# A decoder trunk on one core: 32 of the 44 chunks of the last product as seven-product pairs

## The chip, the core and the metric

The kernel runs on one core of a Trainium2 chip. Its engines are TensorE (PE, matmuls; PEld its weight loads), VectorE (DVE), ScalarE (ACT), GpSimd (POOL) and SyncE (SP); SP and POOL issue the transfers between HBM and on-chip memory, each into a queue of its own. The metric is device time in microseconds. Before: a median of 2108.53 us in three runs (2105.98 to 2113.35).

## The reference

One layer of a decoder trunk on 512 tokens of width 2048, in float32, and a last RMSNorm. The part that matters is the second half of the layer:

```python
def conv_glu_ffn(h, w_gate, w_up, conv_w, conv_b, w_down):
    g = causal_dwconv(h @ w_gate, conv_w, conv_b)
    return (jax.nn.silu(g) * (h @ w_up)) @ w_down
...
x = x + gt2 * conv_glu_ffn(h, ...)
return rmsnorm(x, final_g)
```

`D_FF` is 5632, which is 44 chunks of 128. Every value is split for TensorE into a high and a low part (float32r), and a product is three matmuls: high x high, high x low, low x high. Ahead of this half stand a conditioning vector (`w_ada`, 96 rows of 128 x 2048, each reduced on VectorE), a first RMSNorm, the mixer (pooling, attention, a recurrent branch) and its output projection `w_o`.

## The kernel before, in words

Activations lie feature-major: a tile is 128 features x 512 tokens. Stages follow one another: start, mixer, output projection, four gate/up chunks plainly (`PLAIN`), 40 gate/up pairs, the last product (`w_dn`), the last norm.

**Gate and up as pairs.** A `Pair` takes gate and up chunk i as the two row blocks of a 2 x 2 scheme: features 0 to 1023 and 1024 to 2047 are the two inner blocks, tokens 0 to 255 (`LO`) and 256 to 511 (`HI`) the two column blocks. It needs seven products of half size in place of eight: weights a11, s2, s1, s3, a12, a22, s4 (s1 to s4 are sums made on VectorE) times the forms b11, t2, t1, t3, b21, t4, b22 of the activations, which are made once and stay on chip. `pair_steps` writes the order of a pair by hand: seven windows, one product each; in a window ScalarE casts a later operand to its high part (`high`), VectorE makes the low part (`low`), and banks are copied and added (`kept`, `result`, `c21`, `c11`, `c12`). High and low parts go through a ring of four buffers each, so a cast waits for the product four earlier. The bank A is added to by four products of a pair; each addition waits for ScalarE's copy of what stood there.

**The last product.** The gated tile of each chunk is stored in HBM (`a_d`, POOL). The 44 chunks are cut in groups of 9, 13, 9 and 13 (`FFG`). For a group, each of the 16 output tiles j is one slot: SP loads its weights (`raw_d`), ScalarE and VectorE split them (`wh_d`, `wl_d`), TensorE makes 3 matmuls of 512 columns per chunk, and VectorE adds the bank times a gate into the residual x1b (`down_done`). The next group's gated tiles are loaded and split beside it. The last group runs twice, in token halves of 256 columns, so that the norm of the first half stands beside the second. `drive` loads two slots ahead. The first slot's weights are loaded as `fd_raw`.

The order within an engine is fixed when the program is built; a tile's buffer is given again when the last reader of the old content is done, and the waits follow from that.

## Time and profile before

| | |
|---|---|
| median of 3 runs | 2108.53 us |
| the profiled execution | 2111.79 us, span 2110.0 us |
| TensorE busy | 2044.6 us, 97% |
| VectorE busy | 1481.6 us, 70% |
| ScalarE busy | 879.0 us, 42% |
| granted TensorE clock, mean | 0.992 |
| moved by DMA | 358.80 MB, 170 GB/s in the mean |

Busy time is the union of an engine's instructions; a matmul's row is longer than its distance to the next one, since they are pipelined. The granted clock is given as a share of full speed. The pairs end at about 1599.5 us, and the last product runs from there to 2095.6.

### The profile page before, as it was taken

The numbers are of one execution on the slowest core, as the hardware profiler recorded it, in microseconds if no ns is written. First come the engines' busy times: TensorE is split into PE (matmuls) and PEld (weight loads), VectorE is DVE, ScalarE is ACT, GpSimd is POOL, SyncE is SP. The second block draws the span as 40 slices with busy tenths as digits, with TensorE's granted clock in tenths as the row PEclk, the third lists the DMA queues.
The fourth block names the chain that finished last, engine by engine and source line by source line (L and its number), as shares of the span: only waits on it lengthen the run. The fifth ranks groups of instructions, "written<-read, shape, count | busy, mean of one in ns | idle before, by whom it ended". The sixth has DMA issues, their size and how long they took to land.

```text
span 2110.0 us, 32077 instructions
## 1 busy us (share of the span) xinstructions
PE 2044.6 (97%) x13172; PEld 1858.4 (88%) x13172; DVE 1481.6 (70%) x1850; ACT 879.0 (42%) x1252; POOL 77.5 (4%) x135
## 2 busy tenths in 40 slices
PE   6899999999999999999999999999998999999997
PEld 3678788989877788999999999999997888888997
DVE  7987876777676757887877877878875443344675
ACT  4247432335222634544444544444544231222453
POOL 0001100002000010000000000000000000000000
PEclk9999999999999999999999999999999999999999
DMA  9963466666877235333333334334326543333564
GB/s 360 370 230 100 154 242 229 236 227 219 312 283 281 99 105 181 125 111 125 121 115 125 116 118 128 110 117 134 103 94 236 172 157 96 101 122 120 185 205 135
DMA packets 85846, 358.80 MB, mean 170 GB/s; under 512 B 9793, under 2 KB 16065, under 8 KB 68161
## 3 DMA queue, kind: packets, MB, share of 16 engines
q1 hardware_dynamic: 77442, 336.82, 47.1%
q0 software_dynamic: 8256, 19.93, 2.6%
q8 instruction: 103, 1.69, 0.3%
q14 instruction: 45, 0.37, 0.1%
HBM read 334.69 MB, written 22.02 MB: 169 GB/s over the span
## 4 chain that ended last, share of the span: by engine, by line
PE 70%; DMA 3%; DVE 1%; issue 1%; ACT 0%; DVEq 0%; SPq 0%; ACTq 0%
PE z_d L113 8%; PE z_d L114 8%; PE z_d L115 8%; PE A L938 7%; PE A L939 7%; PE A L937 7%; PE C L937 4%; PE C L938 4%; PE C L939 4%; DMA raw_ada<-in_w_ada 2%; PE B L939 2%; PE B L938 2%; PE B L937 2%; PE z_o L114 2%; PE z_o L115 2%; PE z_o L113 1%
## 5 line engine op out<-in xcount | busy, mean ns | idle before, releaser
L113 PE MATMUL z_d<-a,wh_d 128*128 128x512 f32 (+1 forms) x903 | 308.2, 341 | 0.1
L114 PE MATMUL z_d<-a,wh_d 128*128 128x512 f32 (+1 forms) x903 | 307.8, 341 | 0.0
L115 PE MATMUL z_d<-a,wl_d 128*128 128x512 f32 (+1 forms) x903 | 307.6, 341 | 0.0
L103 ACT CAST wh_d<-raw_d 128x896 fp32r<-128x896 f32 (+3 forms) x158 | 127.1, 805 | 294.1 <-PE z_d L114 293.4
L104 DVE TENSOR_TENSOR wl_d<-raw_d,wh_d 128x896 fp32r<-128x896 f32 (+3 forms) x158 | 145.2, 919 | 148.3 <-ACT wh_d L103 147.1
L126 DVE SCALAR_TENSOR_TENSOR raw_ada<-raw_ada,crep 128x2048 f32<-128x2048 f32 x64 | 147.1, 2299 | 64.8 <-DMA raw_ada<-in_w_ada 64.7
L113 PEld LDWEIGHTS z_d<-a,wh_d 128*128 128x128 f32 x903 | 171.5, 190 | 19.9 <-ACT wh_d L103 0.8
L114 PEld LDWEIGHTS z_d<-a,wh_d 128*128 128x128 f32 x903 | 171.5, 190 | 19.0
L115 PEld LDWEIGHTS z_d<-a,wl_d 128*128 128x128 f32 x903 | 171.3, 190 | 18.8
L1073 DVE SCALAR_TENSOR_TENSOR x1b<-z_d,mod,x1b 128x512 f32<-128x512 f32 (+1 forms) x80 | 51.5, 644 | 87.5 <-PE z_d L115 87.5
L928 DVE TENSOR_TENSOR s1l<-s,s1h 128x1024 fp32r<-128x1024 f32 x40 | 49.0, 1225 | 65.6 <-ACT s1h L923 65.6
L937 PE MATMUL C<-hh_b,s1h 128*128 128x256 f32 x320 | 90.5, 283 | 2.9 <-ACT s1h L923 2.9
L939 PE MATMUL A<-hh_b,a11l 128*128 128x256 f32 x320 | 90.3, 282 | 0.8 <-DVE a11l L928 0.8
L937 PE MATMUL A<-hh_b,a11h 128*128 128x256 f32 x320 | 90.3, 282 | 0.7 <-ACT a11h L923 0.7
L937 PE MATMUL A<-t42h,s2h 128*128 128x256 f32 x320 | 90.7, 283 | 0.0
L938 PE MATMUL A<-t42l,s2h 128*128 128x256 f32 x320 | 90.7, 283 | 0.0
L939 PE MATMUL A<-t42h,s2l 128*128 128x256 f32 x320 | 90.6, 283 | 0.0
L938 PE MATMUL C<-hl_b,s1h 128*128 128x256 f32 x320 | 90.3, 282 | 0.0
L939 PE MATMUL C<-hh_b,s1l 128*128 128x256 f32 x320 | 90.2, 282 | 0.0
L938 PE MATMUL C<-hl_b,s4h 128*128 128x256 f32 x320 | 90.2, 282 | 0.0
L937 PE MATMUL A<-t3h,s3h 128*128 128x256 f32 x320 | 90.2, 282 | 0.0
L939 PE MATMUL B<-hh_b,a12l 128*128 128x256 f32 x320 | 90.2, 282 | 0.0
(652 smaller groups left out, 6258.5 us busy)
## 6 DMA issues: line engine op xcount, KB each, us to landing
a<-in_w_gu SPq DMA_DIRECT2D x160, 512.0 KB, 3.8
raw_ada<-in_w_ada SPq DMA_DIRECT2D x64, 1024.0 KB, 4.9
raw_d<-in_w_dn SPq DMA_DIRECT2D x48, 832.0 KB, 4.4
ada<-in_w_ada SPq DMA_DIRECT2D x32, 1024.0 KB, 7.0
raw_d<-in_w_dn SPq DMA_DIRECT2D x31, 576.0 KB, 3.8
raw_o<-in_w_o SPq DMA_DIRECT2D x16, 1024.0 KB, 5.0
ar<-a_d SPq DMA_DIRECT2D x44, 256.0 KB, 4.7
a_d<-ac POOLq DMA_DIRECT2D x43, 256.0 KB, 3.2
```

Of the source, the lines that this page charges most:

```text
L103: A.copy(h, raw[:, a:b])
L104: V.tensor_tensor(l, raw[:, a:b], h.bitcast(F32), ALU.subtract)
L113: T.matmul(acc, wh, xh, start=start, stop=False)
L114: T.matmul(acc, wh, xl, start=False, stop=False)
L115: T.matmul(acc, wl, xh, start=False, stop=stop)
L126: V.scalar_tensor_tensor(raw, raw, 1.0, crep, op0=ALU.mult, op1=ALU.mult, accum_out=modr[:, n:n + 1])
L928: V.tensor_tensor(l, getattr(self, n), self.w[n][0].bitcast(F32), ALU.subtract)
L937: T.matmul(o, wh[:, w], xh, start=first, stop=False, skip_group_check=True)
L938: T.matmul(o, wh[:, w], xl, start=False, stop=False, skip_group_check=True)
L939: T.matmul(o, wl[:, w], xh, start=False, stop=last, skip_group_check=True)
L1073: V.scalar_tensor_tensor(x1[j][:, c], acc[:, c], mod[:, 80 + j:81 + j], x1[j][:, c], op0=ALU.mult, op1=ALU.add)
```

## The change

Chunks 4 to 35 (32 of 44) of the last product are made by the seven-product scheme too; the other twelve (`REST`: 0 to 3 and 36 to 43) stay plain and run in token halves at the end.

*Forms.* While gate and up run, two gated tiles e and e + 1 are the two inner blocks of a column of seven forms (`Forms`): ScalarE and VectorE make them three steps after chunk e, and POOL stores their high and low parts in HBM (`f_d`), 128 x (4 chunk pairs) x 2 x 256 per form and group. The gated tiles of these chunks are no longer stored.

*Pairs of the last product.* There are four groups of four chunk pairs. In a group, output tiles 2f and 2f + 1 are the two row blocks of a `Down` pair, f from 0 to 7: seven products, each 4 chunks x 3 matmuls of 256 columns. Its weights are blocks of 128 x 512: SP loads a11, a12, a22 and the first term of s1 and s3, and the second term of s1 and s3 is added by a transfer of POOL (`accum_op=ALU.add`), two pairs ahead. The residual tiles are loaded in group 0. The forms of a group are loaded by POOL, 1 MB each, into two sets of buffers (`tm.F`); those of the next group are asked for after the first pair of a group. `down_steps` has the order of `pair_steps`.

*The twelve plain chunks.* In group 3 their gated tiles are loaded and split, two per pair, into the buffers of the forms that are done with (`rest`).

*Smaller things.* Several buffers become single (`t`, `u3`, `u`, `g`), the pool of results `st.m` outlives the gate/up stage, the norm's tiles are cut to its width, the square root's table is no longer loaded ahead of the last norm, the conditioning rows are dealt out differently over the slots (three more in the value products, one fewer in zy3, four fewer in the output projection), and one pooling product moves a slot ahead.

```diff
-FFG = (9, 13, 9, 13)
+DG, DN = 4, 4
+DFIRST, DEND = PLAIN, PLAIN + 2 * DG * DN
+REST = tuple(range(DFIRST)) + tuple(range(DEND, NFF))
+FORMS = ("b11", "t3", "t2", "b21", "t1", "t4", "b22")
...
+    f_d = {(g, n): dr.tile([P, DN, 2, HS], F32R, name=f"f_d_{n}_{g}") for g in range(DG) for n in FORMS}
...
-                              ada=min(kq, 1)))
+                              ada=1))
...
-                     ada=1 if j == 0 else 0 if j >= KC - 2 else 2, post=[lambda acc, j=j: o_done(j, acc)])
+                     ada=1 if j == 1 else 2 if 1 < j < KC - 3 else 0, post=[lambda acc, j=j: o_done(j, acc)])
...
+    class Forms:
+        def __init__(self, e):
+            m = (e - DFIRST) // 2
+            self.i, self.g, self.c, self.t = e, m // DN, m % DN, {}
+            def at(step, window, f, *a):
+                extra.setdefault((e + step, window), []).append(later(f, *a))
+            at(1, 5, self.high, "w", 0, LO)
+            at(2, 0, self.low, "w", ("b11",))
+            at(2, 5, self.high, "x", 1, ALL)
+            at(3, 0, self.low, "x", ("b21", "b22"))
+            at(3, 0, self.sums)
+            at(3, 1, self.high, "y", 0, ALL)
+            at(3, 2, self.low, "y", ("t1", "t3"))
+            at(3, 3, self.high, "z", 1, ALL)
+            at(3, 5, self.low, "z", ("t4", "t2"))
+        def high(self, key, u, c):
+            v = made[self.i + u][:, c]
+            t = tm.fs.tile([P, 2, c.stop - c.start], F32R, tag="fw" if key == "w" else "fs", name=f"f{key}_{self.i}", bufs=1 if key == "w" else 2)
+            A.copy(t[:, 0], v)
+            self.t[key] = t, v
+        def low(self, key, names):
+            t, v = self.t.pop(key)
+            V.tensor_tensor(t[:, 1], v, t[:, 0].bitcast(F32), ALU.subtract)
+            for k, n in enumerate(names):
+                G.dma_start(f_d[self.g, n][:, self.c], t[:, :, k * HS:(k + 1) * HS])
+        def sums(self):
+            e, o = made[self.i], made[self.i + 1]
+            V.tensor_tensor(e[:, LO], e[:, LO], e[:, HI], ALU.subtract)
+            V.tensor_tensor(e[:, HI], o[:, HI], e[:, HI], ALU.subtract)
+            V.scalar_tensor_tensor(o[:, HI], e[:, LO], -1.0, o[:, HI], op0=ALU.mult, op1=ALU.subtract)
+            V.scalar_tensor_tensor(o[:, LO], o[:, HI], -1.0, o[:, LO], op0=ALU.mult, op1=ALU.subtract)
+    for e in range(DFIRST, DEND, 2):
+        Forms(e)
...
+    def load_forms(g, *names):
+        for n in names:
+            Ft[g, n] = tm.F.tile([P, DN, 2, HS], F32R, tag=n, name=f"F{n}_{g}")
+            G.dma_start(Ft[g, n], f_d[g, n])
+    class Down(Pair):
+        n = DN
+        def __init__(self, g, f):
+            self.grp, self.f, self.i, self.w = g, f, f"{g}_{f}", {}
+        def part(self, u, k):
+            return w_dh[2 * self.f + u][:, k, self.grp * DN * P:(self.grp + 1) * DN * P]
+        def load_part(self, n, u, k, bufs):
+            t = st.q.tile([P, DN * P], F32, tag=n, name=f"{n}_{self.i}", bufs=bufs)
+            nc.sync.dma_start(t, self.part(u, k))
+            setattr(self, n, t)
+        def load_s(self):
+            self.load_part("s1", 1, 0, 3)
+            self.load_part("s3", 0, 0, 3)
+            G.dma_start(self.s1, self.part(1, 1), accum_op=ALU.add)
+            G.dma_start(self.s3, self.part(1, 0), accum_op=ALU.add)
+        def load_a(self):
+            self.load_part("a11", 0, 0, 1)
+        def load_b(self):
+            self.load_part("a12", 0, 1, 2)
+            self.load_part("a22", 1, 1, 1)
...
+        def add(self, n, u):
+            j = 2 * self.f + u
+            m = st.neg[:, j:j + 1] if u else mod[:, 80 + j:81 + j]
+            V.scalar_tensor_tensor(x1[j], getattr(self, n), m, x1[j], op0=ALU.mult, op1=ALU.add)
+    def down_steps(p, q, q2, o):
+        q2.load_s()
+        q.load_a()
+        A_ = p.half("A")
+        p.product(A_, "a11", p.x("b11"), True)
+        p.high("s1")
+        p.low("s2")
+        o.c21()
+        o.c11()
+        o.last()
+        m1 = p.kept("m1", A_)
+        p.high("s3")
+        p.low("s1")
+        o.add("u", 1)
+        p.product(A_, "s2", p.x("t2"), False)
+        p.high("a12")
+        o.c12()
+        p.low("s3")
+        o.add("g", 0)
+        C_ = p.half("C")
+        p.product(C_, "s1", p.x("t1"), True)
+        u2 = p.kept("u2", A_)
+        p.high("a22")
+        p.low("a12")
+        p.sum4()
+        p.product(A_, "s3", p.x("t3"), False)
+        q.load_b()
+        q.high_a11()
+        p.low("a22")
+        B_ = p.half("B")
+        p.product(B_, "a12", p.x("b21"), True)
+        u3 = p.kept("u3", A_)
+        p.high("s4")
+        q.sum2()
+        q.low_a11()
+        p.product(A_, "a22", p.x("t4"), False)
+        q.high_s2()
+        p.result("u", HI, u3, C_)
+        p.low("s4")
+        p.last = lambda: p.product(C_, "s4", p.x("b22"), False)
+        p.c21 = lambda: A.copy(p.u[:, LO], A_)
+        p.c11 = lambda: p.result("g", LO, m1, B_)
+        p.c12 = lambda: p.result("g", HI, u2, C_)
+    def down_halves(before):
+        ps_ = [Down(g, f) for g in range(DG) for f in range(KC // 2)] + [ABSENT, ABSENT]
+        p = ps_[0]
+        p.load_s()
+        p.load_a()
+        load_forms(0, "b11", "t2", "t1")
+        ps_[1].load_s()
+        p.load_b()
+        load_forms(0, "t3", "b21", "t4", "b22")
+        p.high("a11")
+        p.sum2()
+        p.low("a11")
+        p.high("s2")
+        before()
+        o = ABSENT
+        for k, p in enumerate(ps_[:-2]):
+            if p.grp == 0:
+                load_x1(2 * p.f)
+                load_x1(2 * p.f + 1)
+            down_steps(p, ps_[k + 1], ps_[k + 2], o)
+            if p.f == 0 and p.grp + 1 < DG:
+                load_forms(p.grp + 1, "b11", "t2", "t1", "t3", "b21", "t4", "b22")
+            if p.grp == DG - 1:
+                rest(p.f)
+            o = p
...
+    rest_a = []
+    def rest(f):
+        if f == 0:
+            st.raw = tm.F.tile([P, 4, S], F32, tag=FORMS[-1], name="rest_raw")
+            rest_a.extend(tm.F.tile([P, 2, 2, S], F32R, tag=n, name=f"rest_{n}") for n in FORMS[:-1])
+        if f in (0, 2, 4):
+            for k in range(4):
+                nc.sync.dma_start(st.raw[:, k], a_d[REST[2 * f + k]])
+        if f < 6:
+            for k in range(2):
+                i = 2 * f + k
+                t, v = rest_a[i // 2][:, i % 2], st.raw[:, i % 4]
+                A.copy(t[:, 0], v)
+                V.tensor_tensor(t[:, 1], v, t[:, 0].bitcast(F32), ALU.subtract)
+                a_h[i], a_l[i] = t[:, 0], t[:, 1]
...
-        for g, nff in enumerate(FFG):
...
+        nr = len(REST)
...
+                s = feature_tile(w_dr[j], f"d{j}_{i}", x, range(nr), c=HALVES[i],
...
```

On POOL, at the end of gate and up, the kernel before has only the stores of the gated tiles, and nothing after them (numbers are the program's own names):

```order
L771 DMA a_d38_148<-ac38_14572 128x512 [waits DMASW6_49,DVE_49]
L771 DMA a_d39_149<-ac39_14805 128x512 [waits DMASW7_49,DVE_49]
L771 DMA a_d40_150<-ac40_15038 128x512 [waits DMASW0_49,DVE_49]
L771 DMA a_d41_151<-ac41_15271 128x512 [waits DMASW1_49,DVE_49]
L771 DMA a_d42_152<-ac42_15495 128x512 [waits DMASW2_49,DVE_49]
L771 DMA a_d43_153<-last_t_15340 128x512 [waits DMASW3_49,DVE_49]
```

In the changed kernel the forms (F, then the form, the group) and the second terms of s1 and s3 (s1, group, pair) stand there, in this order:

```order
L1136 DMA Fb11_0_15949<-f_d_b11_0_122 128x2048 [waits DMASW3_49,PE_49]
L1157 DMA s1_0_0_15941<-in_w_dh 128x512 [waits DMAHW0_49,DMASW4_49,DVE_49]
L1158 DMA s3_0_0_15943<-in_w_dh 128x512 [waits DMAHW5_49,DMAHW1_49,DMAHW6_49,DMASW5_49,Activation_49]
L1136 DMA Ft2_0_15951<-f_d_t2_0_124 128x2048 [waits DMASW6_49]
L1136 DMA Ft1_0_15953<-f_d_t1_0_126 128x2048 [waits DMASW7_49]
...
L1157 DMA s1_0_2_15991<-in_w_dh 128x512 [waits DMAHW1_49,DMASW7_49]
L1158 DMA s3_0_2_15993<-in_w_dh 128x512 [waits DMAHW2_49,DMASW0_49]
L1136 DMA Fb11_1_16117<-f_d_b11_1_129 128x2048 [waits DMASW1_49]
L1136 DMA Ft2_1_16119<-f_d_t2_1_131 128x2048 [waits DMASW2_49]
...
L1136 DMA Fb22_1_16129<-f_d_b22_1_135 128x2048 [waits DMASW7_49]
L1157 DMA s1_0_3_16135<-in_w_dh 128x512 [waits DMAHW7_49,DMASW0_49,DVE_49]
L1158 DMA s3_0_3_16137<-in_w_dh 128x512 [waits DMAHW1_49,DMASW1_49,DVE_49]
```

The first form waits for TensorE; between the parts shown stand the other forms of group 0, the sums of pair 1, one store, and four forms of group 1. The sums of pair 3 stand behind all forms of group 1.

On VectorE the kernel before has, in the second group of the last product, two low parts and one residual add per output tile:

```order
L104 TENSOR_TENSOR wl_d1_5_0_16608<-raw_d1_5_16549,wh_d1_5_0_16607 128x896 [waits DMAHW0_49,Activation_49]
L104 TENSOR_TENSOR wl_d1_5_896_16612<-raw_d1_5_16549,wh_d1_5_896_16611 128x768 [waits PE_49,Activation_49]
L1073 SCALAR_TENSOR_TENSOR x1b_4_15756<-z_d1_4_16615,mod_86,x1b_4_15756 128x512 [waits PE_49]
L104 TENSOR_TENSOR wl_d1_6_0_16664<-raw_d1_6_16605,wh_d1_6_0_16663 128x896 [waits DMAHW1_49,Activation_49]
L104 TENSOR_TENSOR wl_d1_6_896_16668<-raw_d1_6_16605,wh_d1_6_896_16667 128x768 [waits PE_49,Activation_49]
L1073 SCALAR_TENSOR_TENSOR x1b_5_15802<-z_d1_5_16671,mod_86,x1b_5_15802 128x512 [waits PE_49]
L104 TENSOR_TENSOR wl_d1_7_0_16720<-raw_d1_7_16661,wh_d1_7_0_16719 128x896 [waits DMAHW2_49,Activation_49]
L104 TENSOR_TENSOR wl_d1_7_896_16724<-raw_d1_7_16661,wh_d1_7_896_16723 128x768 [waits PE_49,Activation_49]
L1073 SCALAR_TENSOR_TENSOR x1b_6_15848<-z_d1_6_16727,mod_86,x1b_6_15848 128x512 [waits PE_49]
```

The changed kernel has in group 0, where pair 3 starts, this row of instructions (results g, residual adds x1b, the sum s2, low parts, the sum s4 in a12, the s2 of pair 4):

```order
L1182 SCALAR_TENSOR_TENSOR x1b_5_16281<-u_0_2_16423,neg_15939,x1b_5_16281 128x512 [waits DVE_49,Activation_49]
L960 TENSOR_TENSOR g_0_2_16457<-u2_0_2_16361,C_0_2_16348 128x256 [waits PE_49]
L1182 SCALAR_TENSOR_TENSOR x1b_4_16279<-g_0_2_16457,mod_86,x1b_4_16279 128x512 [waits DVE_49]
L1169 TENSOR_TENSOR s2_0_3_16405<-s1_0_3_16135,a11_0_3_16289 128x512 [waits DMASW0_49]
L936 TENSOR_TENSOR s2l_0_3_16454<-s2_0_3_16405,s2h_0_3_16421 128x512 [waits Activation_49]
L936 TENSOR_TENSOR s1l_0_3_16475<-s1_0_3_16135,s1h_0_3_16452 128x512 [waits Activation_49]
L936 TENSOR_TENSOR s3l_0_3_16493<-s3_0_3_16137,s3h_0_3_16473 128x512 [waits DMASW1_49,Activation_49]
L936 TENSOR_TENSOR a12l_0_3_16513<-a12_0_3_16380,a12h_0_3_16490 128x512 [waits DMAHW4_49,Activation_49]
L1173 TENSOR_TENSOR a12_0_3_16380<-a12_0_3_16380,s2_0_3_16405 128x512 [waits DVE_49]
L1169 TENSOR_TENSOR s2_0_4_16553<-s1_0_4_16283,a11_0_4_16437 128x512 [waits DMAHW1_49,DMASW2_49,DVE_49]
L936 TENSOR_TENSOR a22l_0_3_16534<-a22_0_3_16382,a22h_0_3_16511 128x512 [waits DMAHW7_49,PE_49,Activation_49]
L936 TENSOR_TENSOR a11l_0_4_16555<-a11_0_4_16437,a11h_0_4_16532 128x512 [waits PE_49,Activation_49]
```

The sum s2 of pair 3 waits for POOL's transfer (DMASW), and all that follows on VectorE stands behind it.

## Rows read from the trace of the kernel before

**Rows 1.** The page: busy us (share of the span) and instructions of each engine.

```profile
PE 2044.6 (97%) x13172; PEld 1858.4 (88%) x13172; DVE 1481.6 (70%) x1850; ACT 879.0 (42%) x1252; POOL 77.5 (4%) x135
```

**Rows 2.** Windows: five stretches and one across the seam; columns in the first line.

```profile
core 0: us, PE busy (x) PEld busy (x) DVE busy (x) ACT busy (x) POOL busy (x), PEclk, DMA share, GB/s
50.00:100.00 50.00, 42.09 (x176) 30.67 (x175) 49.65 (x65) 14.72 (x21) 0.00 (x0) 1.00 0.98 372
850.00:1450.00 600.00, 600.00 (x5059) 600.00 (x5058) 483.06 (x513) 294.65 (x392) 16.58 (x31) 1.00 0.37 119
1600.00:1620.00 20.00, 15.00 (x58) 11.64 (x59) 12.98 (x19) 11.20 (x18) 0.54 (x1) 0.83 0.95 331
1618.00:1624.00 6.00, 6.00 (x28) 4.98 (x27) 3.44 (x5) 2.49 (x4) 0.00 (x0) 1.00 1.02 392
1620.00:1700.00 80.00, 80.00 (x354) 66.26 (x353) 36.97 (x54) 25.14 (x40) 0.00 (x0) 1.00 0.59 192
1980.00:2090.00 110.00, 110.00 (x918) 109.95 (x917) 73.17 (x115) 55.84 (x86) 0.00 (x0) 1.00 0.58 185
```

**Rows 3.** Timeline of TensorE at the seam and the end: start us, us, instruction [idle].

```profile
1597.84 0.28 PE L939 MATMUL C<-hh_b,s4l 128*128 128x256 f32 x1
...
1599.26 0.28 PE L939 MATMUL C<-hh_b,s4l 128*128 128x256 f32 x1
...
1604.94 0.79 PE L113 MATMUL z_d<-a,fd_h 128*128 128x512 f32 x1 [5.40 <-ACT fd_h L1110]
...
1607.24 0.63 PE L115 MATMUL z_d<-a,fd_l 128*128 128x512 f32 x1
...
1607.66 0.63 PE L113 MATMUL z_d<-a,fd_h 128*128 128x512 f32 x1
...
1609.19 0.39 PE L115 MATMUL z_d<-a,fd_l 128*128 128x512 f32 x1
...
1609.42 0.40 PE L113 MATMUL z_d<-a,fd_h 128*128 128x512 f32 x1
...
2095.29 0.28 PE L115 MATMUL z_d<-a,wl_d 128*128 128x256 f32 x1
```

**Rows 4.** Groups of VectorE by form: operands, xcount | busy us, mean ns.

```profile
L104 DVE TENSOR_TENSOR wl_d<-raw_d,wh_d 128x768 fp32r<-128x768 f32 x48 | 46.0, 958 | 81.7 <-ACT wh_d L103 81.7
...
L1073 DVE SCALAR_TENSOR_TENSOR x1b<-z_d,mod,x1b 128x512 f32<-128x512 f32 x48 | 36.0, 750 | 72.9 <-PE z_d L115 72.9
...
L1100 DVE TENSOR_TENSOR a<-ar,a 128x512 fp32r<-128x512 f32 x44 | 29.5, 689 | 15.7 <-ACT a L1099 15.6
...
L952 DVE TENSOR_TENSOR g<-m,B 128x256 f32<-128x256 f32 x39 | 16.4, 421 | 12.5 <-PE B L939 12.5
...
L833 DVE TENSOR_TENSOR x<-x,x 128x256 f32<-128x256 f32 x8 | 3.3, 418 | 0.0
```

**Rows 5.** Groups of ScalarE by form.

```profile
L103 ACT CAST wh_d<-raw_d 128x768 fp32r<-128x768 f32 x48 | 40.1, 835 | 92.0 <-PE z_d L114 91.8
...
L1099 ACT CAST a<-ar 128x512 fp32r<-128x512 f32 x44 | 26.9, 620 | 22.9 <-DMA ar<-a_d 21.7 <-PE C L939 0.4 <-PE z_d L115 0.2
...
L946 ACT COPY m<-A 128x256 f32<-128x256 f32 x40 | 14.6, 364 | 0.0
```

**Rows 6.** The page: transfers by queue, KB each, median us from issue to landing.

```profile
raw_ada<-in_w_ada SPq DMA_DIRECT2D x64, 1024.0 KB, 4.9
...
ar<-a_d SPq DMA_DIRECT2D x44, 256.0 KB, 4.7
...
a_d<-ac POOLq DMA_DIRECT2D x43, 256.0 KB, 3.2
...
x_d<-x POOLq DMA_DIRECT2D x16, 256.0 KB, 6.8
```

**Rows 7.** What TensorE waited for, 440 to 720 us: total, times, longest.

```profile
PE z_o L115 <- DVE wl_o L104: 3.9, 4, 1.6
```

**Rows 8.** Groups of GpSimd: its issue of a store.

```profile
L771 POOL DMA_DIRECT2D a_d<-ac x43 | 23.2, 541 | 791.8 <-DVE ac L969 771.4 <-DVE ac L782 20.4
```

More of the change, by code (lines that the diff above doesn't have):

```diff
@@ L90, in trunk @@
     x1_d = [dr.tile([P, S], F32, name=f"x1_d{j}") for j in range(KC)]
-    a_d = [dr.tile([P, S], F32, name=f"a_d{i}") for i in range(NFF)]
+    a_d = {i: dr.tile([P, S], F32, name=f"a_d{i}") for i in REST}
+    f_d = {(g, n): dr.tile([P, DN, 2, HS], F32R, name=f"f_d_{n}_{g}") for g in range(DG) for n in FORMS}
     def pieces(n, unit=P):
@@ L932, in product @@
             wh, wl = self.w.pop(n)
-            for c in range(HC):
+            for c in range(self.n):
                 w = slice(c * P, (c + 1) * P)
                 xh, xl = xs(c)
-                first, last = start and c == 0, c == HC - 1
+                first, last = start and c == 0, c == self.n - 1
                 T.matmul(o, wh[:, w], xh, start=first, stop=False, skip_group_check=True)
@@ L992, in pair_steps @@
         o.c11()
+        also(0)
         o.last()
@@ L1006, in pair_steps @@
         o.store2()
+        also(2)
         C_ = p.half("C")
@@ L1022, in pair_steps @@
         o.gated()
+        also(4)
         B_ = p.half("B")
@@ L1036, in pair_steps @@
         q.sum3()
+        also(6)
         def last():
@@ L1057, in strassen @@
             if q is ABSENT:
-                for n in "gut":
-                    setattr(p, n, st.end.tile([P, S], F32, name=f"last_{n}"))
-            pair_steps(p, q, o)
+                p.t = st.m.tile([P, S], F32, tag="last", name="last_t", bufs=1)
+            pair_steps(p, q, o, lambda k, i=i: [f() for f in extra.get((i, k), ())])
             o, p = p, q
@@ new lines, in load_x1 @@
+    def load_x1(j):
+        x1[j] = xy.tile([P, S], F32, tag="xy", name=f"x1b_{j}")
+        nc.sync.dma_start(x1[j], x1_d[j])
+    def down_halves(before):
[23 more added lines that the diff above has]
+            o = p
+        o.c21()
+        o.c11()
+        o.last()
+        o.add("u", 1)
+        o.c12()
+        o.add("g", 0)
@@ new lines, in down_slots @@
+        nr = len(REST)
+        x = lambda: ([a_h[i] for i in range(nr)], [a_l[i] for i in range(nr)])
+        for i in range(2):
+            for j in range(KC):
+                s = feature_tile(w_dr[j], f"d{j}_{i}", x, range(nr), c=HALVES[i],
+                                 post=[lambda acc, i=i, j=j: (down_done(j, acc, HALVES[i]), norms[3, i].add(x1[j]))])
+                if i:
+                    s.post.append(later(last_gain, j))
+                if i == 1:
+                    if j == 1:
+                        s.pe.append(normed("sum", 3, 0))
+                    elif j == 3:
+                        s.pe.append(normed("spread", 3, 0))
+                    if 3 <= j < 11:
+                        s.post.append(later(last_scale, 0, range(2 * (j - 3), 2 * (j - 3) + 2)))
```

162 lines of the change are left out of this document (58 added, 104 removed).

## Prediction

> **What bounds the kernel now.** I read the busy shares first: TensorE works 97% of the span [rows 1]. Then stretches: from 850 to 1450, where the seven-product pairs of gate and up run, it has no idle time in 600 us, and the plain stretches of the last product are as full [rows 2]. So time there is number of matmuls times their pitch, and a gain must come from fewer matmuls. Third, the timeline at the seam into the last product: the last matmul of the pairs starts at 1599.26, the first of the last product at 1604.94, 5.40 us idle, and then 512-column matmuls stand 0.42 us apart where later they stand 0.23 apart [rows 3]; the granted clock of that stretch is 0.83 [rows 2], so TensorE runs at 1.2 GHz there after the pause, about 9 matmuls, 1.9 us lost. That seam is short because it asks for little: one 576 KB block of weights and some 256 KB tiles. The changed kernel asks for a lot there, and that decides my forecast.
>
> The profiled execution took 2111.79 us, 3.3 over the median of 2108.53. I sum differences in the profiled one and add them to the median.
>
> **The work taken out.** 256-column matmuls stand 0.1186 us apart (600 us / 5059 [rows 2]; the timeline gives 1.42 / 12 = 0.118 [rows 3]). For 512 columns the timeline gives 0.23 [rows 3] and the stretch from 1620 gives 80 / 354 = 0.226 with some records missing [rows 2]; I take 0.228. Before: 31 chunks x 16 x 3 = 1488 wide and 13 x 16 x 2 x 3 = 1248 narrow: 339.3 + 148.0 = 487.3 us. With the 1.9 us this is 489.2; the rows give 1604.94 to 2095.41 = 490.5 [rows 3]. After: 32 pairs of output rows (eight in each of four groups) x 7 products x 12 = 2688, and 12 x 96 = 1152, all narrow: 3840 x 0.1186 = 455.4. **-31.9 us.** The seven products save an eighth of the multiplications, but a narrow matmul costs 4% more per column.
>
> **The seam, and what stands in POOL's queue.** Let 0 be the end of the last gate/up matmul. POOL's first load, form b11 of group 0, waits for that matmul, and so does SP's first weight block: the new tiles lie where its operands lay. So nothing is fetched ahead. A group has seven forms of 1.05 MB (128 x 8 KB). In POOL's order all seven of group 0, the sums of pairs 0 to 2, then all seven of group 1 stand ahead of the sums s1 and s3 of pair 3. Up to those two sums POOL's queue carries 14 x 1.049 + 8 x 0.262 + one store of 0.262 = 17.0 MB. SP meanwhile issues 41 loads of 256 KB before the first that waits for pair 3's sum: 25 weight blocks and all 16 residual tiles, 10.7 MB. Together 27.8 MB.
>
> How fast? With the DMA engines full the kernel moves 372 GB/s (50 to 100), 392 (1618 to 1624) and 331 at this seam [rows 2]. I take 380: 73 us, and with 2 us for issue and landing s1 of pair 3 is there at 75. Then s2 (0.69), its high part (0.62) and its low part (0.69) [rows 4, 5], 2.2 with the hand-overs, before TensorE can go on in pair 3. It has long done pairs 0 to 2: b22 of group 0, 8.4 MB down POOL's queue with 6.8 to 8 MB of SP's beside it, lands at about 43, and two pairs of 84 x 0.1186 = 9.96 us end by 63. After 77 there are 34 products of 1.42 us left in the group (6 of pair 3, 28 of pairs 4 to 7), 48.4, and 1.9 for the clock after the pause as at the seam before. Group 0 ends at 127.5 where its 56 products alone take 79.7: 47.8 us lost, in place of 5.4 + 1.9 = 7.3. **+40.5.**
>
> Bounds. Below: SP gets no further than 26 of its 41 loads (6.8 MB), rate 392: 23.8 MB, 61 us, so the loss is 36 and the term +28. Above: the rate of the seam, 331, and each sum moving its bytes twice (2.1 MB more): 29.9 MB, 90 us, loss 65, term +57. That transfers of one queue land one after the other no row shows by itself; what load does to one is seen in POOL's stores of 256 KB, 3.2 us in gate and up and 6.8 in the output projection, and 1 MB alone takes 4.9 [rows 6].
>
> The Trainium skill ("DMA: Bandwidth & Descriptors", section "Where 436 GB/s comes from") holds that loads from HBM end at about 358 GB/s and not at the 435 of the SBUF side. The rows stand a little above it; by 358 the bytes would take 78 us, and the forecast would be 5 us later.
>
> No row here has a transfer that adds into its target. The Trainium skill ("Collectives: The Full Stack", section "The bandwidth ceiling: the fold count and why AG ≠ RS ≠ AR") says that such an add needs two source reads, which halved the rate of a ring there. By it the eight sums would count twice, 5.5 us more, an estimate from that page.
>
> **Later groups.** The forms of the next group are asked for as the last pair lets go of each buffer. SP needs 5 blocks per pair, 1.31 MB in 9.96 us = 132 GB/s; that leaves 248 for about 6.8 MB still queued when the group's second product starts: 27 us, and the sum behind them is due at about 29. Without stall at 380; at 331 some 4 us late, and in the last group, where SP also fetches plain tiles (52 GB/s more), 4 at either rate. **+3** (0 to 10).
>
> **VectorE in a pair of the last product.** Seven low parts and two sums of 512 columns at 0.69, three results at 0.42, two residual adds at 0.75 [rows 4] are 9.0 us of 9.96. Followed through its queue with ScalarE's casts at 0.62 and copies at 0.36 [rows 5], each low part is there at least two products before its use, and each copy of the A bank is done about 0.3 us before the bank is added to. So nothing waits, but there is no more room: in the last group two splits of a plain tile per pair put 1.4 us more on VectorE (10.3 us) and a cast beside the copies. **+3** (0 to 6). If the sum of a pair is late by 1 us, all 13 instructions behind it on VectorE are late too, and so is TensorE.
>
> **Into the plain chunks.** The first cast of the plain weights goes into memory that the last pair product reads, so it waits for its last matmul: hand-over, cast 0.84 [rows 5], then result, add and low part 0.42 + 0.75 + 0.96 [rows 4] before the third matmul: 2.3 us, and 1.9 for the clock. **+4** (2 to 5).
>
> **The gate and up pairs.** VectorE is busy 483 / 600 of a 19.9 us pair, 16.1 us [rows 2]. Every second pair gets a 256- and three 512-column splits and four 256-column sums: 0.4 + 3 x 0.69 + 4 x 0.43 = 4.2 us, mostly in one of two. The full one stands at 19.9 of 19.9, the next makes it good, and each low part has about two products of 2.84 us in hand. ScalarE (295 / 600) has room. **+1** (0 to 8). The forms' stores, 1.8 MB in two pairs, are 46 GB/s where 119 flow [rows 2].
>
> **Conditioning rows moved.** TensorE waits 3.9 us in four places for weights split late in the output projection [rows 7]; five rows fewer there may return some of it, three more in the value products may cost as much. **-1** (-4 to +3). The square root's table load, no longer taken ahead, lies beside the second token half.
>
> **Sum.** -31.9 + 40.5 + 3 + 3 + 4 + 1 - 1 = +18.6. 2108.5 + 18.6 = **2127 us**. With each term at its lower end it is -31.9 + 28 + 2 - 4 = -6, with each at its upper +57; not all fall together, so the likeliest case spans 2112 to 2148.
>
> **Rivals.** *Faster:* the sums don't stand behind group 1's forms, because the engines serve several transfers of one queue at once or SP's loads flow freely. For it: POOL's issue takes 0.54 us per transfer [rows 8], so 14 forms are not asked for at once. Against it: the order on POOL is fixed, and the sums of pair 3 are issued last. Then TensorE waits only for group 0's own forms: 8.4 MB at 372 is 24 us with the issue, by when 7 products are done, and the other 49 take 69.7: group 0 ends at 94, 14 us lost and 1.9. With the other terms (10) the total is -31.9 + 8.6 + 10 = -13: 2095. It decides when pair 3's sum is there before about 35.
> *Cancelled:* SP's residual tiles come after the sums and the other terms stay near zero: -31.9 + 28 + 4 = about 2109. For it: part of SP's 41 loads waits for pair 2's own progress.
> *Much slower:* adding transfers run at half speed or less and VectorE has no room in every pair: 32 pairs x 0.7 us more = 22 on top: 2150. For it: 9.0 of 9.96 us; against it: gate and up run at 16.1 of 19.9 without a wait.
>
> **Chances.** Forecast 0.55, much slower 0.17, cancelled 0.15, faster 0.13. A difference under 0.3% (6.3 us) can't be told from none here. Faster by more 0.13, within 0.13, slower by more 0.74. The range for 8 in 10 runs from 2100, between the faster and the cancelled case, to 2160, past the much slower one.
>
> **What would show it.** Right: TensorE idle in some seven pieces in the 45 us behind the seam, each ended by a POOL load; one idle piece of 10 to 17 us before pair 3's s2 product, ended through VectorE by the sum; DMA share above 0.9 for 70 us; then pairs of 9.96 us. Wrong: pairs 3 to 7 following without that piece; 12 x 0.1186 us not holding for a product; TensorE waiting in gate and up for copies of its banks.

## The result and the profile after

The changed kernel took a median of 2166.8 us (2163.3 to 2167.6, four runs) against 2109.6 (2106.0 to 2113.4) before: a ratio of 1.0268 (95% interval 1.0246 to 1.0290), 57 us slower. The forecast was 2127 with a range from 2100 to 2160: the sign was right, the size was not. The profiled execution took 2166.81 us, 55.0 more than that of before.

TensorE is busy for 5.5 us less than in [rows 1], in a span 55 us longer:

```profile
PE 2039.1 (94%) x14276; PEld 1905.3 (88%) x14276; DVE 1662.2 (77%) x2252; ACT 980.2 (45%) x1538; POOL 206.1 (10%) x307
```

The windows that answer to [rows 2] (columns in the first line) say where. Gate and up (850 to 1450), full before, lost 9.2 us of 600. Behind the seam, from 1620 on, the DMA engines are full (1.05 and more) for 60 us and TensorE works about half of the time. From 1700 the pairs run as forecast, but short pieces are missing again around 1850 and 1950.

```profile
core 0: us, PE busy (x) PEld busy (x) DVE busy (x) ACT busy (x) POOL busy (x), PEclk, DMA share, GB/s
850.00:1450.00 600.00, 590.84 (x4930) 587.69 (x4929) 515.39 (x618) 309.92 (x440) 71.32 (x105) 1.00 0.53 149
1620.00:1640.00 20.00, 8.46 (x36) 7.46 (x36) 6.77 (x10) 4.67 (x9) 8.73 (x13) 0.67 1.08 347
1640.00:1660.00 20.00, 15.37 (x108) 14.72 (x108) 5.90 (x10) 4.81 (x10) 4.05 (x7) 0.85 1.07 379
1660.00:1680.00 20.00, 8.93 (x60) 8.65 (x60) 7.64 (x13) 4.05 (x9) 0.85 (x1) 0.83 1.07 392
1680.00:1700.00 20.00, 9.99 (x60) 9.78 (x60) 6.73 (x11) 3.57 (x9) 3.41 (x4) 0.66 0.82 223
1700.00:1760.00 60.00, 59.57 (x488) 59.47 (x489) 49.05 (x83) 32.88 (x67) 13.16 (x18) 0.97 0.81 221
1840.00:1860.00 20.00, 17.93 (x139) 17.73 (x138) 13.36 (x24) 8.37 (x18) 2.55 (x4) 0.91 1.06 388
1940.00:1960.00 20.00, 19.01 (x147) 18.60 (x146) 17.43 (x31) 11.89 (x25) 3.39 (x4) 0.93 0.86 209
```

TensorE's timeline at the seam (answering to [rows 3]; in brackets the idle time and what ended it):

```profile
1612.27 0.28 PE L947 MATMUL C<-hh_b,s4l 128*128 128x256 f32 x1
...
1621.90 0.58 PE L945 MATMUL A<-Fb,a11h 128*128 128x256 f32 x1 [9.35 <-ACT a11h L931]
...
1631.17 0.55 PE L945 MATMUL A<-Ft,s2h 128*128 128x256 f32 x1 [6.04 <-DMA Ft<-f_d_t]
...
1641.53 0.55 PE L945 MATMUL A<-Ft,s3h 128*128 128x256 f32 x1 [4.96 <-DMA Ft<-f_d_t]
...
1663.08 0.58 PE L945 MATMUL A<-Ft,a22h 128*128 128x256 f32 x1 [5.23 <-ACT u L954]
...
1687.83 0.58 PE L945 MATMUL A<-Ft,s3h 128*128 128x256 f32 x1 [15.82 <-ACT u L954]
...
1700.43 0.49 PE L945 MATMUL A<-Ft,s2h 128*128 128x256 f32 x1 [2.60 <-ACT s2h L931]
```

The pieces at 1631 and 1641 end with a form, as forecast. The longest, 15.82 us, stands before the s3 product of pair 2, not before the s2 of pair 3 (2.60).

Where the 55.0 us are, from the starts of the first and last matmul of each stage in the two timelines, with 1.4237 us a product:

| stage | before | after | difference | forecast |
|---|---|---|---|---|
| up to the last plain gate/up matmul | 795.21 | 788.16 | -7.05 | -1 |
| from there to the first pair's first matmul | 1.11 | 6.48 | +5.4 | 0 |
| gate/up pairs, first to last matmul | 802.9 | 817.6 | +14.7 | +1 |
| last product: work | 487.3 | 455.5 | -31.8 | -31.9 |
| loss at the seam and in group 0 | 7.3 | 58.5 | +51.2 | +40.5 |
| loss in groups 1 to 3 | - | 20.4 | +20.4 | +3 and +3 |
| rest of the last product (into the plain chunks) | 1.4 | 3.5 | +2.1 | +4 |
| behind the last plain matmul | 16.5 | 16.6 | +0.1 | 0 |

### The profile page after: what moved, and what is told of

Read it like the earlier page. It is cut to its first block, busy times and chain, and to the rows that moved or that the text cites. A ratio compares the mean times of both kernels' runs of the same rounds, so it can differ in the third digit from the quotient of the medians.

```text
span 2165.0 us, 35728 instructions
## 1 busy us (share of the span) xinstructions
PE 2039.1 (94%) x14276; PEld 1905.3 (88%) x14276; DVE 1662.2 (77%) x2252; ACT 980.2 (45%) x1538; POOL 206.1 (10%) x307
## 4 chain that ended last, share of the span: by engine, by line
PE 62%; DMA 8%; DVE 2%; ACT 2%; issue 1%; SPq 0%; DVEq 0%; POOL 0%; ACTq 0%; POOLq 0%
PE A L945 10%; PE A L946 9%; PE A L947 9%; PE C L945 4%; PE C L946 4%; PE C L947 4%; DMA a<-in_w_dh 3%; DMA raw_ada<-in_w_ada 2%; PE B L946 2%; PE B L945 2%; PE B L947 2%; PE z_d L120 2%; PE z_d L119 2%; PE z_d L118 2%; PE z_o L119 1%
## 5 line engine op out<-in xcount | busy, mean ns | idle before, releaser
L936 DVE TENSOR_TENSOR s1l<-s,s1h 128x1024 fp32r<-128x1024 f32 (+1 forms) x72 | 71.1, 988 | 47.6 <-ACT s1h L931 47.6
L931 ACT CAST s2h<-s 128x1024 fp32r<-128x1024 f32 (+1 forms) x72 | 61.9, 860 | 71.0 <-PE B L946 42.3
L931 ACT CAST s1h<-s 128x1024 fp32r<-128x1024 f32 (+1 forms) x72 | 61.8, 858 | 69.1 <-PE A L946 67.9
L936 DVE TENSOR_TENSOR s4l<-a,s4h 128x1024 fp32r<-128x1024 f32 (+1 forms) x72 | 70.9, 985 | 27.4 <-ACT s4h L931 27.4
L946 PE MATMUL A<-hl_b,a11h 128*128 128x256 f32 x320 | 91.0, 284 | 0.0
L947 PE MATMUL A<-t42h,a22l 128*128 128x256 f32 x320 | 90.2, 282 | 0.0
L947 PE MATMUL A<-t3h,s3l 128*128 128x256 f32 x320 | 90.2, 282 | 0.0
L947 PE MATMUL C<-hh_b,s4l 128*128 128x256 f32 x320 | 90.2, 282 | 0.0
L946 PE MATMUL B<-hl_b,a12h 128*128 128x256 f32 x320 | 90.2, 282 | 0.0
L946 PE MATMUL A<-t42l,a22h 128*128 128x256 f32 x320 | 90.2, 282 | 0.0
```

What stands on the lines that cost most here:

```text
L931: A.copy(h, getattr(self, n))
L936: V.tensor_tensor(l, getattr(self, n), self.w[n][0].bitcast(F32), ALU.subtract)
L946: T.matmul(o, wh[:, w], xl, start=False, stop=False, skip_group_check=True)
L947: T.matmul(o, wl[:, w], xh, start=False, stop=last, skip_group_check=True)
```

## The experiments

Each ratio is to the kernel before on the same chip; the changed kernel's is 1.0268. "Last product" here is the time from the last gate/up matmul to the first of the twelve plain chunks, 398.8 us in the changed kernel, of which 318.9 are its matmuls; "gate/up" is that of the table. Both are of one profiled execution. In e1 and e9, which move nothing in the last product, it took 395.9 and 401.0, so 3 us there tell nothing; and the 5.23 and 15.82 us in pairs 1 and 2 of group 0 were 11.17 and 10.76 in e1: their sum holds, each alone does not.

**e1: one cast in written order.** The order within an engine is the builder's, and differs from the code's; `keep_in_program_order` keeps an instruction where the code has it. In the changed kernel ScalarE's cast of form z stands ahead of the next pair's s1 cast and m copy. ScalarE's timeline there:

```profile
1177.15 0.62 ACT L1089 CAST fy<-ac 128x512 fp32r<-128x512 f32 x1
1178.79 1.05 ACT L931 CAST s2h<-s 128x1024 fp32r<-128x1024 f32 x1 [1.01 <-PE B L946]
1186.65 0.62 ACT L1089 CAST fz<-ac 128x512 fp32r<-128x512 f32 x1 [6.81 <-DMA f_d_b<-fx]
1187.17 1.04 ACT L931 CAST s1h<-s 128x1024 fp32r<-128x1024 f32 x1
...
1189.33 0.37 ACT L954 COPY m<-A 128x256 f32<-128x256 f32 x1
```

The cast waits for the store of form x to leave its buffer (two of them); the m copy stands behind, and TensorE's next addition to bank A started at 1189.76. Waits of 850 to 1490 us (total, times, longest):

```profile
ACT fz L1089 <- DMA f_d_b<-fx: 80.5, 16, 6.8
...
PE A L945 <- ACT m L954: 9.8, 12, 2.3
```

```diff
-            A.copy(t[:, 0], v)
+            c = A.copy(t[:, 0], v)
+            if key == "z":
+                tc.keep_in_program_order(c)
```


> Only the cast of form tile z (ScalarE, gate and up) is kept in the order in which the code is written; in the changed kernel it stands ahead of the next pair's s1 cast and m copy and waits for the store of form tile x (80.5 us in 16 times, max 6.8). Theory A (ScalarE's queue is held by that wait, the copy of bank A stands behind it, TensorE waits): TensorE's waits for the m copy in gate and up (9.8 us, 12 times) fall under 1 us, the stage (817.8 us from the first to the last pair matmul, 803.1 before the change) takes 803 to 805, and the time falls from 2166.8 to 2153 (2151 to 2156). Theory B (VectorE and ScalarE simply have too much work in every second pair): the waits stay, only their place moves: 2163 or more.

Ratio 1.0192 (1.0162 to 1.0221). Gate/up took 801.5, and TensorE had no wait there:

```profile
850.00:1450.00 600.00, 600.00 (x5059) 600.00 (x5058) 531.20 (x635) 321.33 (x451) 71.48 (x106) 1.00 0.51 153
```

VectorE and ScalarE do more in these 600 us than in the changed kernel, and nothing waits: theory A.

**e2: residual tiles in written order.** SP's queue is the only one that changes.

```diff
-        nc.sync.dma_start(x1[j], x1_d[j])
+        tc.keep_in_program_order(nc.sync.dma_start(x1[j], x1_d[j]))
```


> Only SP's order changes: the residual tiles x1b 4 to 15 stand two ahead of each pair, as the code is written, in place of all ahead of pair 2's a22 block. Theory A (SP's queue: pair 2's a12 and a22 land late behind the residual tiles, their casts wait 11.10 and 6.62 us on ScalarE and TensorE 15.8 us before pair 2's s3 product): ten tiles, 2.6 MB, less ahead of a22 are 7 us at 380 GB/s, more if the clock comes back earlier: 2158 (2152 to 2162), the 15.8 us piece at most 9. Theory B (my forecast: pair 3's sums behind the forms of group 1 on POOL's queue end the stall): POOL's queue is as before, a gain of 3 us at most: 2164 to 2167.

Ratio 1.0188 (1.0155 to 1.0220); last product 387.4, 11.4 less. TensorE's waits in pairs 1 and 2 fell from 21.1 us to 10.6: 2.55 in place of 15.82 before pair 2's s3, 3.8 before its a22. Theory A. Gate/up, where no instruction was moved, took 810.7 in place of 817.6: that stage's waits (4.9 us here) vary, 810.5 to 820.4 over the profiled executions with the z cast ahead, and about 7 us of the gain are that. (The four runs of e2 go from 2146.3 to 2158.0, and the profiled one is the lowest.)

In the changed kernel SP's queue at the seam (start, us, issues) and ScalarE's beside it read:

```profile
1642.29 11.36 SPq L1237 DMA_DIRECT2D x1b<-x_d  x5
1655.39 0.33 SPq L1150 DMA_DIRECT2D a<-in_w_dh  x1
1658.42 12.97 SPq L1237 DMA_DIRECT2D x1b<-x_d  x5
1674.30 3.51 SPq L1150 DMA_DIRECT2D s<-in_w_dh  x2
1679.62 3.12 SPq L1150 DMA_DIRECT2D a<-in_w_dh  x3
```

```profile
1668.19 0.37 ACT L954 COPY m<-A 128x256 f32<-128x256 f32 x1
1679.66 0.62 ACT L931 CAST a12h<-a 128x512 fp32r<-128x512 f32 x1 [11.10 <-DMA a<-in_w_dh]
1686.89 0.62 ACT L931 CAST a22h<-a 128x512 fp32r<-128x512 f32 x1 [6.62 <-DMA a<-in_w_dh]
1687.41 0.37 ACT L954 COPY u<-A 128x256 f32<-128x256 f32 x1
```

Pair 2's a12 and a22 come behind all the residual tiles, their casts hold ScalarE, and the u copy that TensorE needs stands behind them; the bank it copies was complete at 1670.4 (the s2 product began at 1669.01). Two things make them so late. A load issued between 1635 and 1662 takes 18 to 24 us to land, where such a weight block takes 5.6 in the median of the whole run. And SP issues a load just after the one eight before it has landed (1645.46 after 1645.45, 1664.76 after 1664.70), so the ten residual tiles hold its queue from 1642.29 to 1674.30.

**e3: group 1's forms later.**

```diff
-            if p.f == 0 and p.grp + 1 < DG:
+            if p.f == (3 if p.grp == 0 else 0) and p.grp + 1 < DG:
```


> The seven forms of group 1 (7.3 MB) are asked for after pair 3 of group 0 in place of after pair 0; the other groups as they were. Theory A (bytes in flight behind the seam: everything that pairs 1 and 2 wait for shares the DMA engines with these 7.3 MB): 7.3 MB at 380 GB/s are 19 us, of which some comes back where group 1 begins about 40 us after they are asked for: 2150 (2145 to 2156); TensorE's waits of 5.2 and 15.8 us in pairs 1 and 2 shrink to under 8 in sum. Theory B (only the sums of pair 3 stand behind them): the waits in pairs 1 and 2 stay as they are, since they are for SP's blocks behind the residual tiles, and only the 2.6 us before pair 3's s2 goes: 2162 to 2165.

Ratio 1.0167 (1.0145 to 1.0188); last product 385.0, 13.8 less. The 5.23 and 15.82 us in pairs 1 and 2 became 3.03 and 0.75, others of 2.5 and 3.2 came in pairs 4 and 5. Theory A: forms and SP's blocks share the engines. Gate/up took 810.5, again some 7 us of the gain.

**e4: casts of the last product in written order.** The same pin on `Down`'s casts and on those of the plain tiles.

```diff
+        def high(self, n):
+            h = st.r.tile([P, self.n * P], F32R, tag="wh", name=f"{n}h_{self.i}")
+            tc.keep_in_program_order(A.copy(h, getattr(self, n)))
+            self.w[n] = [h]
```

> Every ScalarE cast of the last product (weights and plain tiles) is kept in written order, behind the copy of bank A that the code writes ahead of it; in the changed kernel the a22 cast stands ahead of the u2 copy and a plain tile's cast ahead of the m copy. Theory A (a cast that waits for a transfer holds the copy, TensorE waits for the copy): in groups 1 to 3 the pieces of 3.71, 2.07, 1.83, 3.05 and 0.74 us and the half-speed time behind each (20.4 us lost there in all) fall to 8 or less, some 3 us go at the seam: 2152 (2148 to 2158). Theory B (the transfers themselves are too late, by more than the two products between copy and use, 2.85 us): TensorE then waits at the product that needs the cast, and the time stays: 2163 to 2168.

Ratio 1.0200 (1.0174 to 1.0226); last product 387.3, 11.5 less; gate/up took 820.4. TensorE's waits in groups 1 to 3 were, in the changed kernel and here:

```profile
PE A L945 <- ACT u L954: 8.2, 5, 3.7
PE A L945 <- ACT m L954: 3.8, 2, 3.0
PE A L945 <- ACT s2h L931: 2.6, 1, 2.6
```

```profile
PE A L945 <- ACT u L954: 9.0, 3, 5.7
```

So both theories hold, in different places. Behind the plain tiles' casts (the last group) the waits are gone: A. At the starts of groups a22 was late by more than the two products between, so the wait moved to a later product: B. (The 2.6 us in the first list is the seam's, at 1700.43.)

**e5: addresses at the seam.** Group 0's first forms and the weight blocks are laid where the last gate/up pair is done early: an own buffer per form and parity of group, taken in a chosen order (`SLOTS`), and the weight pool ahead of the ring.

```diff
+    SLOTS = ("b11_1", "t2_1", "t1_1", "b11_0", "t3_1", "b21_1", "t4_1",
+             "t2_0", "t1_0", "b21_0", "t4_0", "t3_0", "b22_0", "b22_1")
-    st.r = pool(dps, "ring2", 4, "right")
     st.q = pool(dps, "q2", 1, "right")
+    st.r = pool(dps, "ring2", 4, "right")
```


> Only addresses change: group 0's forms lie where the last gate/up pair is done first (b11, t2, t1, t3 under operands of its early products, not of its last one), and the weight blocks of the last product under the gate/up weight blocks and not under the ring of their casts. Theory A (at the seam nothing is fetched ahead only because of where the tiles lie): the first product starts 2 to 5 us after the last gate/up matmul in place of 9.5, the two waits of 6.0 and 5.0 us for forms t2 and t3 go; the waits of 5.2 and 15.8 us for SP's blocks behind the residual tiles shrink or stay: 2140 to 2155. Theory B (the bytes behind the seam set its end, wherever they begin): what is gained ahead is lost again in pairs 1 and 2: 2158 to 2166.

Ratio 1.0212 (1.0189 to 1.0235); last product 392.1, only 6.7 less: theory A failed as put, and the time, 2157.9 us, lies at the lower edge of B. GpSimd's timeline tells why:

```profile
1597.65 0.89 POOL L1163 DMA_DIRECT2D s<-in_w_dh  x1
...
1608.69 0.84 POOL L1163 DMA_DIRECT2D s<-in_w_dh  x1 [1.65 <-DMA s<-in_w_dh]
1609.42 0.98 POOL L1164 DMA_DIRECT2D s<-in_w_dh  x1
1609.95 1.02 POOL L1142 DMA_DIRECT2D Fb<-f_d_b  x1
```

The last gate/up matmul started at 1607.16. Six sums now stood ahead of the first form on GpSimd's queue and waited for SP's blocks one after another; the form was asked for some 14 us after the last matmul that reads what lay there (four products of 2.85 us stand behind that one in gate and up). The first product came 13.8 us after the last gate/up matmul, and 21 us were lost in pair 1 behind a late a22.

**e6, e7, e8: together.** e6 has the orders of e1 to e4, the residual tiles behind a pair's own loads, two buffers for a22, and pair 0's loads ahead of pair 1's; e7 adds the addresses of e5; e8 also pins SP's weight loads.

```diff
         p.load_a()
+        load_forms(0, "b11")
+        p.load_s()
+        p.load_b()
+        load_forms(0, "t2", "t1", "t3", "b21", "t4", "b22")
+        ps_[1].load_s()
```


> All order changes at once, addresses as in the changed kernel: form tile z, the casts and the residual tiles in written order (residual tiles asked for after a pair's weights), group 1's forms asked for after pair 3, pair 0's loads and forms ahead of pair 1's, and two buffers for a22. Alone the first four took 14.7 (1.6 of it by chance in gate and up), 14.6, 20.2 and 10.5 us. Theory A (three causes: the z cast in gate and up, late blocks at the seam, casts ahead of copies later): about 14 in gate and up, 15 to 20 at the seam, 10 in the groups: 2123 (2115 to 2130). Theory B (the bytes at the seam are one sum, order only shifts the wait): 14 + 10 and no more than 8 at the seam: 2133 to 2140.

> The orders of e6 and the addresses of e5 together. Theory A: the seam loses no more than 15 us of its 58.5, the groups 5 of 20.4, gate and up nothing: 2166.8 - 14 - 43 - 15 = about 2095 (2088 to 2105), faster than before the change (2108.5). Theory B: the seam stays bound by bytes at 30 or more: 2110 or more.

> As e7, and SP's weight loads of the last product too in strictly written order, so that a load that waits for its buffer holds those behind it. Theory A (what comes too early hurts more than what is held): the forms at the seam come sooner and it is 0 to 5 us better than e7. Theory B (SP's queue held by a buffer makes blocks late in every pair): 5 to 15 us worse than e7, with waits for a22 or a12 in every group.

e6: 2121.0 us, 1.0045 (1.0026 to 1.0063), gate/up 801.5, last product 364.8: theory A. e7: 2115.2, 1.0005 (0.9987 to 1.0023), 363.6: the addresses added little, theory A missed by 20 us and B held; the first form was still behind the sums (12.6 us of wait for it). e8: 2112.1, 0.9994 (0.9980 to 1.0008), 361.7: not the loss of theory B, but its interval overlaps that of e7. With SP strict, the first two forms stood ahead of the sums and the first product came 2.15 us after the last gate/up matmul. What was gained there was lost again in waits of 5.9 us in pair 0, 5.5 in pair 1 and 4.4 in pair 5, with the DMA engines at 1.00 to 1.08 up to 1690. So addresses helped only where the queue's order let the transfer use them. That the bytes of seven forms asked for at once are the bound behind both is argued here; e10 and e12 test it.

**e9: the first block of gate and up.** In the changed kernel the first pair's a11 lies under weights that the last plain matmul reads; before, under weights done half a chunk earlier. The pool of results, now first on that side, had moved it.

```diff
+        st.q.tile([P, HC * P], F32, tag="s1", name="s1_first")
         f = st.first = Pair(PLAIN)
```


> Only addresses in the gate and up stage change: the tile of s1 is given the lowest place of the weight pool, so that the first pair's a11 block moves from under the second half of the last plain weights' low part (read by the last matmul of the plain chunks) to under the first half, as it lay before the change. Theory A (that address is why the first gate/up pair starts 6.1 us after the last plain matmul where it was 0.73): the wait for a11h falls from 5.8 or 6.1 us to under 1.5, and the time by 4 to 6 (the wait and the half-speed matmuls behind it): 2161 (2159 to 2164). Theory B (the loads of the first pair are late because the DMA engines are busy there with the forms of the activations): the wait stays above 4 us, 2164 or more.

Ratio 1.0208 (1.0177 to 1.0239). The first pair started 2.56 us after the last plain matmul in place of 6.48, its wait 2.17 in place of 6.10: theory A, by two thirds. Gate/up's 812.6 is most of the rest of the gain.

**e10, e11: what beats both.** On e8: one form of the next group per pair; pair 1's sums ahead of the last three forms; the first plain weights and e9's block under operands done early. In e10 the residual is added by GpSimd's transfers in groups 1 and 2, in e11 loaded in group 0.

```diff
-            if p.f == 0 and p.grp + 1 < DG:
-                load_forms(p.grp + 1, "b11", "t2", "t1", "t3", "b21", "t4", "b22")
+            if p.f and p.grp + 1 < DG:
+                load_forms(p.grp + 1, ("b11", "t2", "t1", "t3", "b21", "t4", "b22")[p.f - 1])
```


> On e8 (2112.1, before the change 2113.8 on the same chip) five more changes: the next group's forms are asked for one per pair, not seven at once; the residual is left out of group 0 (its result is written, not added) and added to it by transfers of POOL in groups 1 and 2, two halves of 2.1 MB; pair 1's sums stand ahead of the last three forms of group 0; the plain weights' first block and the first gate/up block lie under operands that are done early. Theory A (what is left of the stalls is bytes that need not be there at the time): pair 1's s2 (5.5 us), the 4.4 us behind a late residual tile, the 3 us at each group's start, the 4.8 into the plain chunks and the 5.8 at the first pair fall under 8 in sum: 2112 - 16 = 2096 (2090 to 2102), 0.8% faster than before the change. Theory B (DMA engines at 1.06 of their time for 90 us behind the seam: less is moved then, but adding transfers cost more than loads): gain of 5 to 8 only: 2104 to 2108.

> As e10, but the residual tiles are loaded by SP in group 0, two ahead of each pair, and added there, as in the changed kernel. Theory A (4.2 MB in the 80 us of group 0 come to 11 us at 380 GB/s, where forms and weights already need 70 us): group 0 stalls 4 to 10 us more than in e10: 2100 to 2106. Theory B (the 16 residual tiles fit in beside forms that come one per pair): within 2 us of e10.

e10: 2085.5 us (2081.6 to 2087.3), ratio 0.9859 (0.9832 to 0.9887), 1.4% faster than the kernel before, and below the 2090 to 2102 of theory A. e11: 2086.3, 0.9869 (0.9840 to 0.9897): theory B, where the residual is read made no difference. e10's windows:

```profile
850.00:1450.00 600.00, 600.00 (x5058) 600.00 (x5058) 530.60 (x631) 321.30 (x452) 71.44 (x105) 1.00 0.52 153
1600.00:1620.00 20.00, 14.19 (x101) 13.87 (x101) 8.87 (x16) 6.48 (x13) 3.10 (x4) 0.83 1.08 340
1620.00:1700.00 80.00, 80.00 (x677) 80.00 (x676) 63.62 (x114) 43.50 (x88) 19.26 (x25) 1.00 1.00 284
1700.00:1900.00 200.00, 199.82 (x1684) 199.61 (x1683) 171.09 (x291) 113.45 (x230) 53.42 (x67) 1.00 1.03 293
```

From 1620 on TensorE is full with the DMA engines full beside it: the same bytes (425.1 MB in either kernel), in time. The last product takes 334.4, of 318.9 of matmuls; 15.0 of the loss stand in group 0, ahead of 1620.

**e12: the spread.** The diff of e10, on the changed kernel. The loads of the forms are kept in written order too, so it is not quite the spread alone: the written order puts pair 0's sums ahead of the first form, and the first product came 17.3 us after the last gate/up matmul in place of 9.6.

> The changed kernel with one change: the next group's forms are asked for one after each pair, not seven at once after the first pair. Theory A (the waits at the starts of groups 1 to 3 come from seven forms that share the DMA engines with the pair's weight blocks): the last product, 537.9 us from the last gate/up matmul to the last plain one, loses the 12 us that e3 showed for group 1's forms at the seam and some 8 to 12 us more in groups 1 to 3: 512 to 518; the pieces of 3.7, 2.1 and 1.8 us before s3 are gone, those of 3.1 and 0.7 us behind a plain tile's cast stay; time 2140 (2134 to 2147). Theory B (those waits come from the single a22 buffer and the order of the casts, whatever the forms do): only e3's gain, 524 to 528, 2146 to 2153.

2137.3 us, ratio 1.0118 (1.0071 to 1.0166). From the last gate/up matmul to the last plain one it took 506.6 in place of 537.9, more than theory A gave. Groups 1 and 2 have no wait left. In group 3 those of 1.9 and 3.2 us behind plain tiles' casts are, and two of 0.3 and 0.6. Of the single changes it is the largest.

## Why the prediction was wrong, point by point

**The step that failed** is that I priced waits by the room on the engines. In a pair of the last product: "each low part is there at least two products before its use, and each copy of the A bank is done about 0.3 us before the bank is added to. So nothing waits". In gate and up: "ScalarE (295 / 600) has room". I followed engine times only. ScalarE's queue also holds casts that wait for transfers, and the builder had put them ahead of the copies. The one mechanism, a late transfer, a cast that waits for it, the copy behind the cast, TensorE, showed in three places (e1, e2, e4). Of the 36.4 us by which the sum missed (+55.0 for +18.6), 13.7 are gate and up, 14.4 groups 1 to 3 and 10.7 the seam; the other terms come to -2.4.

*Gate and up, +14.7 for +1 (0 to 8).* I had even written down "TensorE waiting in gate and up for copies of its banks" as what would prove me wrong, and then looked for room on VectorE, not at what the z cast waits for. There was room: e1.

*Groups 1 to 3, +20.4 for +3 (0 to 10) and +3 (0 to 6).* I had summed the bytes and not looked at how few microseconds they come in. A group's 56 products take 79.7 us. Here are groups 1 and 2 of the changed kernel, the same two together in e12, and group 3 in e4, each from its first matmul to the next group's (in e4 to the plain chunks, which is 1.0 us more; columns as in the windows above):

```profile
1750.59:1836.19 85.60, 81.87 (x674) 81.45 (x673) 67.04 (x114) 43.36 (x88) 17.03 (x24) 0.98 0.89 258
1836.19:1923.39 87.20, 83.31 (x674) 82.89 (x673) 67.23 (x114) 43.26 (x88) 17.60 (x23) 0.96 0.86 244
1733.87:1893.36 159.49, 159.49 (x1347) 159.49 (x1346) 133.89 (x226) 86.90 (x176) 35.00 (x46) 1.00 0.96 278
1920.85:2001.56 80.71, 79.91 (x675) 79.70 (x673) 71.85 (x124) 48.28 (x99) 8.59 (x10) 1.00 0.68 194
```

So the 5.9 and 7.5 us lost in groups 1 and 2 are the burst: seven forms at once on the blocks of two or three pairs. (e4, which keeps the burst, still loses 9.1 and 3.4 there.) The 7.0 lost in group 3, which loads plain tiles and no forms of a next group, are the casts of these tiles, which waited for their loads ahead of the copies. The last group's row on ScalarE:

```profile
1937.18 0.62 ACT L1286 CAST rest_t<-rest_raw 128x512 fp32r<-128x512 f32 x1 [3.30 <-DMA rest_raw<-a_d]
1937.70 0.61 ACT L931 CAST s3h<-s 128x512 fp32r<-128x512 f32 x1
1938.22 0.36 ACT L954 COPY m<-A 128x256 f32<-128x256 f32 x1
```

*The seam, +51.2 for +40.5 (28 to 57).* The size of the stall was right, its place was not. I had the sums of pair 3 there 75 us after the last gate/up matmul, "long" after pairs 0 to 2. POOL issued them at 1657.57 and 1660.79, and from issue to landing they took:

```profile
DMA to landing us min/median/max: 22.8/23.4/24.0
```

So they were there some 69 and 71 us after it, and TensorE did not wait for them. TensorE did resume 75.4 us after it (1687.83 less 1612.39), but in pair 2, for the a12 and a22 behind SP's residual tiles. These stood behind about the same bytes as the sums; that the time came out for other blocks is in part luck. Of the 56 products of the group 39 were left and not 34, 7.1 us; 2.6 us were waited in pair 3 on top, where VectorE made the sum s2 only at 1698.98, behind its residual adds; the slow clock behind these last two pieces cost 4.6 where I had 1.9. I had counted those tiles as bytes, and not asked what stands behind them on SP.

*The sums that add.* I priced them like loads and had double in the upper bound alone. In 30 us without forms (1885 to 1915; packets, MB, share of 16 engines):

```profile
q1 hardware_dynamic: 2167, 3.95, 41.7%
q0 software_dynamic: 863, 1.57, 31.8%
```

The second queue carries nothing but these sums there: 20.3% per MB against 10.6% for loads, 1.9 times. It is not the queue, for with forms in it (1660 to 1680, 20 us) it is no dearer than the loads above, 8.8% per MB when scaled to 30 us:

```profile
q0 software_dynamic: 956, 6.07, 79.8%
```

By these rows the seam's eight sums (2.1 MB) kept the engines busy for some 6 us more than I had in the middle value, an estimate. The Trainium skill ("Collectives: The Full Stack", section "The bandwidth ceiling: the fold count and why AG ≠ RS ≠ AR") holds of the add in a ring's ReduceScatter that it needs two source reads; the 1.9 of this trace fits that. In the middle of a group they delay nothing (groups 1 and 2 of e12).

*Conditioning rows, -1 (-4 to +3), in truth two terms.* The earlier stages ended 7.05 us sooner, 1.9 of it by the first matmul of the output projection (512.5 for 514.4). Four rows fewer stand in the projection, not the five that I counted, and its four waits [rows 7] fell to two:

```profile
PE z_o L120 <- DVE wl_o L109: 0.9, 2, 0.6
```

But 5.4 were lost again at once, 3.9 of them by the first block's new address (e9), which I hadn't considered.

*Right:* the work (pairs at 9.97 us, a product at 12 x 0.1186); nothing fetched ahead of the seam; DMA engines full for 70 us (share 1.06 from 1613 to 1682, at 362 GB/s where I took 380); the plain chunks' start. The rival "much slower" gave a nearer number, 2150, from another mechanism: its adds at half speed held, but VectorE without room in every pair, from which its 22 us came, e1 and e10 refute: at 531 of 600 and 171 of 200 us TensorE is full.
